# Keeping the weight rooms across a phase change, and starting loads, transposes and last sums at other places, in a one-core decoder layer

## The chip, the cores and the metric

One Trainium2 chip, one of its cores. The time is that of one launch in device microseconds (us); a lower time is better. Five engines work side by side, each through its own instructions in order: TensorE (PE in the profile, with PEld for its weight loads), VectorE (DVE), ScalarE (ACT), GpSimd (POOL) and SyncE (SP). SP computes nothing here: it issues loads from DRAM, one after the other. POOL computes a little and issues most stores. All transfers run on the same 16 DMA engines.

## The reference, cut to what matters

One decoder layer, in fp32, for a prompt of 2048 rows of 1024 columns and for a small group of samples (8 requests of 4 new rows each, with states and caches that are read from DRAM).

```python
def decoder_layer(x, s_gla, s_ssm, conv_buf, mk, mv, lw):
    m, s_gla, s_ssm, conv_buf = mixer(rmsnorm(x, lw['ln_mix_pre']), s_gla, s_ssm, conv_buf, lw)
    h = x + rmsnorm(m, lw['ln_mix_post'])
    a = cross_attend(rmsnorm(h, lw['ln_xa_pre']), mk, mv, lw['w_xq'], lw['w_xo'])
    h = h + rmsnorm(a, lw['ln_xa_post'])
    hf = rmsnorm(h, lw['ln_ffn_pre'])
    f = (jax.nn.silu(hf @ lw['w_gate']) * (hf @ lw['w_up'])) @ lw['w_down']
    h = h + rmsnorm(f, lw['ln_ffn_post'])
    return h, s_gla, s_ssm, conv_buf
```

The mixer (`mixer`) is an input projection, a gated linear attention, an SSD scan with a short convolution, and an output projection `w_out`. The attention (`cross_attend`) projects with `w_xq`, takes a softmax over 256 memory rows of 4 heads, and projects with `w_xo`. The feed-forward part has 2816 columns.

## The kernel before, in words

**Two phases.** Phase A (up to about 886 us) is the mixer without its output projection, in four blocks of 512 rows, and it leaves the mixed rows in DRAM (`mixT`). Phase B is everything behind it, and nearly all of the change lies there.

**Phase B is a row of passes.** `o` is the output projection, `s` the scores (with the query projection folded into the memory keys), `v` the values (folded with `w_xo`), each of 8 units, one for 256 rows. Then three passes `g` (gate and up projections, for three blocks of rows; 22 units each, one for 256 columns of gate or of up) and four passes `d` (parts of the down projection, 8 units each). A unit is one 2x2 block product by the Strassen-Winograd scheme: seven block products, in the order p0, C11, p3, p2, C12, C22, C21. In this text a unit is named by its pass and number, so g0.00 is the first unit of the first `g` pass, and one of its seven products is a *place*. At each place the kernel first emits the product's matmuls (12 for four inner blocks, three for each, because every fp32 operand is split into a high and a low half: L127 high x high, L128 and L129 the cross terms), into accA, accB or accC, and then the small steps that belong to other work.

**What a product needs.** The operand that PE loads as its weights comes from `Unit`: SP loads 1 MB or less into one of two `raw` buffers (L1521, L1530), DVE makes the Strassen sums (L1489), ACT the high half (L1507) and DVE the low half (L1509), four places ahead. The operand that streams comes from `Pieces`: it is loaded through three `st` buffers, and made into a high half by ACT (L1571, `r<-st`) and a low half by DVE (L1575), in *rooms* r0 to r6 (r7 too in `d`). A pass makes its seven products once and uses them in all its units, so a room comes free at the last unit of the pass, one at each place, and the next pass's pieces are made there ("coming").

**The rooms before.** In `o`, `s` and `v` a room has 2 x 2048 fp32 in each partition, in `g` and `d` 2 x 1536. `change_rooms` closes the pool "rx" and opens the pool "rf" of the smaller ones after the last product of v0.07. So no piece of g0 is made during v0.07 (`p = None` there), and g0.00 makes two pieces at each place.

**Work beside the products.** `posts` are generators that carry the rows of a finished unit on: `after_mix`, `after_scores`, `after_values` (norms, the residual, and `turned`: eight transposes on PE, L1691, of the rows `u` that ACT makes at L1730), `after_down` and `after_direct`. All are stepped once at each place (`tick`). `aux` and `back` hold side work that is stepped at so many tenths of a place (RATES): in `aux` `weight_sums` (Strassen sums of the next passes' weights: two loads on SP, then DVE L1410 to L1414, then stores on POOL) and `samples_down` (the down projection of the samples, with loads `w`), in `back` `samples` (mixer, states and attention of the samples, in g0 and g1). `pin` keeps each engine's instructions of phase B in the order in which this code is written, so a wait at the head of an engine's queue holds up all that is written behind it.

**The end.** In the last two units, d3.06 and d3.07, the sums of the other parts and the residual rows (`yp`, `hX`: two tensors of 512 KB for each 128 rows) are loaded by SP into free rooms when d3.06 begins (z and h), and added when the products are taken out of the accumulators (L1876). The unit before still adds by accumulating DMAs on POOL. Result rows `y` are a ring of 7 buffers.

## Time and profile before

| what | value |
|---|---|
| time, median of 3 runs | 3017.38 us (3011.25 to 3018.79) |
| profiled execution | 3010.56 us, its span 3008.8 us, mean TensorE clock 0.98 |
| instructions in the span | 42293 |
| PE busy | 2842.5 us, 94% of the span |
| DVE, ACT, POOL busy | 2086.4, 1523.9, 551.9 us |
| bytes moved | 529.89 MB, a mean of 176 GB/s |

How to read what is quoted below. A line of the *waits* names an engine and its line, the work that it waited for, and then the sum of the waits in us, their number, and the longest. A line of the *windows* gives a stretch of time in us and its length; then the busy time and the number of instructions of PE, PEld, DVE, ACT and POOL; then the clock that PE was granted (1.00 is full speed), the mean busy share of the 16 DMA engines, and GB/s. A line of a *timeline* gives the start, the length, the engine, the line and operation, the tile written and the tile read. A line of the *DMA issues* gives the number, the KB of one and the median us from issue to landing. Since PE is busy for 94% of the span, a stall is to be looked for in a stretch, not in the average.

### The profile page before, as it was taken

The numbers are of one execution on the slowest core, as the hardware profiler recorded it, in microseconds if no ns is written. First come the engines' busy times: TensorE is split into PE (matmuls) and PEld (weight loads), VectorE is DVE, ScalarE is ACT, GpSimd is POOL, SyncE is SP. The second block draws the span as 40 slices with busy tenths as digits, with TensorE's granted clock in tenths as the row PEclk, the third lists the DMA queues.
The fourth block names the chain that finished last, engine by engine and source line by source line (L and its number), as shares of the span: only waits on it lengthen the run. The fifth ranks groups of instructions, "written<-read, shape, count | busy, mean of one in ns | idle before, by whom it ended". The sixth has DMA issues, their size and how long they took to land.

```text
span 3008.8 us, 42293 instructions
## 1 busy us (share of the span) xinstructions
PE 2842.5 (94%) x15207; PEld 2385.9 (79%) x15207; DVE 2086.4 (69%) x3915; ACT 1523.9 (51%) x3044; POOL 551.9 (18%) x753
## 2 busy tenths in 40 slices
PE   8999989999988989999698999999999999999997
PEld 8887777787866778877588988888999995587875
DVE  7676676766657687777587777767678884566576
ACT  5454543645356686767544434434455552445453
POOL 2142341211222221034213000010000000011122
PEclk9999999999999999999799999999999999999998
DMA  7355543242267675567556356774243345768788
GB/s 247 115 157 171 166 129 117 78 130 85 88 221 251 222 262 199 189 192 236 186 194 216 136 176 215 256 262 142 96 154 119 127 144 180 243 130 196 161 214 244
DMA packets 154769, 529.89 MB, mean 176 GB/s; under 512 B 19360, under 2 KB 22608, under 8 KB 143040
## 3 DMA queue, kind: packets, MB, share of 16 engines
q1 hardware_dynamic: 93168, 331.75, 34.4%
q0 software_dynamic: 49152, 170.46, 18.6%
q10 hardware_dynamic: 12240, 24.99, 2.6%
q8 instruction: 120, 1.97, 0.3%
q14 instruction: 89, 0.73, 0.1%
HBM read 373.04 MB, written 154.09 MB: 175 GB/s over the span
## 4 chain that ended last, share of the span: by engine, by line
PE 56%; issue 16%; DMA 7%; DVE 6%; ACT 5%; POOL 2%; POOLq 0%; DVEq 0%; ACTq 0%; SPq 0%
PE accA L127 7%; PE accA L128 7%; PE accA L129 7%; PE accC L127 4%; PE acc L127 4%; PE accC L128 4%; PE accC L129 4%; PE acc L128 4%; PE acc L129 4%; PE accB L127 2%; PE accB L128 2%; PE accB L129 2%; PE mx L1916 1%; PE mx L1691 1%; ACT r L1571 1%
## 5 line engine op out<-in xcount | busy, mean ns | idle before, releaser
L127 PE MATMUL accA<-r,s 128*128 128x512 f32 (+2 forms) x1792 | 643.5, 359 | 39.5 <-ACT r L1571 13.5
L129 PE MATMUL accA<-r,s 128*128 128x512 f32 (+2 forms) x1792 | 631.7, 353 | 7.7 <-DVE s L1509 7.0
L128 PE MATMUL accA<-r,s 128*128 128x512 f32 (+2 forms) x1792 | 632.2, 353 | 6.9 <-DVE r L1575 6.8
L127 PEld LDWEIGHTS accA<-r,s 128*128 128x128 f32 x1792 | 340.5, 190 | 115.8 <-ACT r L1571 18.1
L1507 ACT ACTIVATE s<-sum 128x512 fp32r<-128x512 f32 (+2 forms) x488 | 289.4, 593 | 264.1 <-DVE sum L1489 102.0
L128 PEld LDWEIGHTS accA<-r,s 128*128 128x128 f32 x1792 | 340.7, 190 | 40.9 <-DVE r L1575 12.0
L129 PEld LDWEIGHTS accA<-r,s 128*128 128x128 f32 x1792 | 340.7, 190 | 39.2 <-DVE s L1509 9.6
L127 PE MATMUL accC<-r,s 128*128 128x512 f32 (+2 forms) x896 | 324.9, 363 | 18.7 <-ACT r L1571 6.8
L1509 DVE TENSOR_TENSOR s<-sum,s 128x512 fp32r<-128x512 f32 (+2 forms) x488 | 309.2, 642 | 35.0 <-ACT s L1507 31.7
L129 PE MATMUL accC<-r,s 128*128 128x512 f32 (+2 forms) x896 | 317.8, 355 | 7.4 <-DVE s L1509 7.4
L128 PE MATMUL accC<-r,s 128*128 128x512 f32 (+2 forms) x896 | 317.4, 354 | 1.0 <-DVE r L1575 0.9
L1509 DVE TENSOR_TENSOR s<-raw,s 128x512 fp32r<-128x512 f32 (+2 forms) x366 | 235.4, 643 | 59.0 <-ACT s L1507 57.5
L1507 ACT ACTIVATE s<-raw 128x512 fp32r<-128x512 f32 (+2 forms) x366 | 218.2, 596 | 53.2 <-PE accC L129 50.9
L121 ACT ACTIVATE whi<-wraw 128x1024 fp32r<-128x1024 f32 (+2 forms) x148 | 137.1, 941 | 197.1 <-PE acc L128 100.2
L127 PEld LDWEIGHTS accC<-r,s 128*128 128x128 f32 x896 | 171.5, 191 | 63.0 <-issue 11.2
L122 DVE TENSOR_TENSOR wlo<-wraw,whi 128x1024 fp32r<-128x1024 f32 (+2 forms) x148 | 167.5, 1142 | 59.2 <-ACT whi L121 58.5
L129 PEld LDWEIGHTS accC<-r,s 128*128 128x128 f32 x896 | 171.7, 192 | 25.1 <-DVE s L1509 9.1
L1575 DVE TENSOR_TENSOR r<-st,r 128x1024 fp32r<-128x1024 f32 (+2 forms) x133 | 136.6, 1029 | 76.1 <-ACT r L1571 75.6
L128 PEld LDWEIGHTS accC<-r,s 128*128 128x128 f32 x896 | 171.7, 192 | 16.7 <-DVE r L1575 2.1
L127 PE MATMUL acc<-xh,whi 128*128 128x512 f32 (+1 forms) x464 | 168.3, 364 | 8.4 <-ACT xh L282 8.3
L135 POOL TENSOR_TENSOR rs<-ms,nhalf 128x1 f32<-128x1 f32 (+4 forms) x125 | 105.8, 848 | 329.2 <-DVE ms L133 322.1
L129 PE MATMUL acc<-xh,wlo 128*128 128x512 f32 (+1 forms) x464 | 164.2, 355 | 1.7 <-DVE wlo L122 1.7
(644 smaller groups left out, 5775.4 us busy)
## 6 DMA issues: line engine op xcount, KB each, us to landing
raw<-in_w_gu_dram SPq DMA_DIRECT2D x66, 1024.0 KB, 5.0
wraw<-in_w_in_fm_dram SPq DMA_DIRECT2D x52, 512.0 KB, 3.7
wraw<-in_w_in_tm_dram SPq DMA_DIRECT2D x48, 512.0 KB, 3.7
yp<-y POOLq DMA_DIRECT2D x48, 512.0 KB, 6.8
raw<-aT SPq DMA_DIRECT2D x24, 768.0 KB, 5.2
st<-in_w_down_dram SPq DMA_DIRECT2D x34, 512.0 KB, 6.9
aT<-og POOLq DMA_DIRECT2D x22, 768.0 KB, 4.3
hX<-y POOLq DMA_DIRECT2D x32, 512.0 KB, 5.4
```

What stands on the lines that cost most here:

```text
L121: last[0] = nc.scalar.activation(hi[:, cs], raw[:, cs], AF.Copy)
L122: nc.vector.tensor_tensor(lo[:, cs], raw[:, cs], f(hi)[:, cs], op=ALU.subtract)
L127: nc.tensor.matmul(ps, lhsT=wh, rhs=ah, start=start, stop=False, skip_group_check=more)
L128: nc.tensor.matmul(ps, lhsT=wh, rhs=al, start=False, stop=False, skip_group_check=more)
L129: nc.tensor.matmul(ps, lhsT=wl, rhs=ah, start=False, stop=stop, skip_group_check=more)
L135: nc.gpsimd.tensor_tensor(out=rs[:rows, :cols], in0=ms[:rows, :cols], in1=nhalf[:rows, :cols], op=ALU.pow)
L1507: nc.scalar.activation(h3, v, AF.Copy)
L1509: return lambda: nc.vector.tensor_tensor(l3, v, f(h3), op=ALU.subtract)
L1571: nc.scalar.activation(hi, v, AF.Copy)
L1575: nc.vector.tensor_tensor(lo, v, f(hi), op=ALU.subtract)
L1691: nc.tensor.transpose(ps[kt // 4][:, kt % 4 * P:(kt % 4 + 1) * P], u[:, kt * P:(kt + 1) * P], ident)
L1916: nc.tensor.matmul(ps[g0:g0 + 32], lhsT=s_f[:, kt].rearrange("p h t -> p (h t)"), rhs=ws.popleft(), start=kt < 4, stop=kt >= FT - 4, tile_ ...
```

## The change

Every part of the change moves, keeps or splits work; the matmuls are the same in number and size.

- **Rooms.** `change_rooms` is gone. One pool "rp" of seven rooms of 2 x 1536 stays open for all of phase B. In `o`, `s` and `v`, whose halves need 2048, the missing 1024 of each room stand in a second tile `e` in the pool "rx", which is closed when g0 begins (the `wide` form). Pieces of g0 are made during v0.07, one at each place, like those of any other pass.
- **Transposes.** `after_mix` and `after_values` yield once more before `turned`, and the ring `u` has four buffers in place of three.
- **weight_sums** yields four times in place of two between its loads and its sums.
- **Samples.** `back` is stepped at 6 tenths of a place in `g` instead of 5. The convolution state is loaded earlier, and the convolution is split by yields. The sample value rows go through DRAM (`svs`) instead of staying in a buffer. The loads of `cache_k` and `cache_v` are issued two ahead.
- **d0.** When `d` begins, its pool places the room r7 and the five `w` buffers first, so that the tiles which follow lie elsewhere: `y` no longer lies where `og` (the output tile of `g`) was, and the first `w` buffer does. So ScalarE's first write of `y` (L1878) waits for PE alone, and SP's first `w` load (L1905) waits for the stores of `og`; before it was the other way round.
- **The end.** All eight loads of `yp` and `hX` are issued when d3.05 begins.

```diff
+    rp = ctx.enter_context(tc.tile_pool(name="rp", bufs=1, reuse_waits="tile"))
+    rx = rctx.enter_context(tc.tile_pool(name="rx", bufs=1, reuse_waits="tile"))
...
-    RW = 2048
+    RW = 1536
@@ weight_sums
-        yield
-        yield
+        for _ in range(4):
+            yield
@@ Pieces.larger
-                self.at[i] = r[:, 0:RW], r[:, RW:2 * RW]
+                if self.wide:
+
+                    e = rx.tile([P, 1024], F32R, name=f"e{k}")
+                    self.at[i] = [r[:, c * 1024:(c + 1) * 1024] for c in range(2)], [r[:, 2048:3072], e]
+                else:
+                    self.at[i] = r[:, 0:RW], r[:, RW:2 * RW]
@@ after_mix
         u = yield from after_rows(j, m, y, ss, "ln_mix_post", a["x"])
+        yield
         turned(u)
@@ after_values
         u = yield from after_rows(j, m, y, ss, "ln_xa_post", None)
+        yield
         turned(u, gff)
@@ sample_mixer
+        cvo = mt_([P, 8, NR, 3], "cvo")
+        nc.gpsimd.dma_start(out=cvo, in_=a["state_conv"])
+        yield
+        yield
+        yield
...
-        cvo = mt_([P, 8, NR, 3], "cvo")
-        nc.gpsimd.dma_start(out=cvo, in_=a["state_conv"])
+        yield
...
+            if i % 2:
+                yield
@@ the passes
-    RATES = {"o": (0, 9), "s": (0, 9), "v": (0, 0), "g": (5, 4), "d": (0, 8)}
+    RATES = {"o": (0, 9), "s": (0, 9), "v": (0, 0), "g": (6, 4), "d": (0, 8)}
@@ enter
         if kind == "g":
             if i == 0:
+                rctx.close()
                 pg = fctx.enter_context(tc.tile_pool(name="pg", bufs=1, reuse_waits="tile"))
...
             pd = ctx.enter_context(tc.tile_pool(name="pd", bufs=1, reuse_waits="tile"))
+
+            pd.tile([P, 2 * RW], F32R, name="r7")
+            pd.tile([P, 512], F32, name="w", bufs=5)
             gain_row(pd, "ln_ffn_post")
@@ the loop over the products
-                if n + 2 >= len(work):
-
-                    if n + 2 == len(work):
+                if n + 3 == len(work):
...
+                    for j in (g + 1, g + 2):
+                        z, h = [rooms.pop(0), rooms.pop(0)], [rooms.pop(0), rooms.pop(0)]
+                        for m in range(2):
+                            nc.sync.dma_start(out=z[m], in_=yp[j][:, m * D:(m + 1) * D])
+                            nc.sync.dma_start(out=h[m], in_=hX[rows(j, m)])
...
-        if i == 6 and n + 1 < len(work) and begins[n + 1] and k + 1 == XG:
-            change_rooms()
-            for _ in range(2):
-                coming.step()
...
-        if p and p is coming and work[cur][0] + 1 == XG:
-            p = None
         if p:
             p.larger()
         tick()
         if p:
             p.smaller()
-            if p.k == XG:
-                p.step()
```

**ScalarE, from the end of v0.07 into g0.00.** `r<-st` are the pieces of g0 (two to a product, the number is that of the room's tile), `sg<-accA` is the first product of g0.00 taken out, `u<-y` the rows that are transposed next, and `u<-mx` the transposed rows read back. Before:

```order
L1682 ACTIVATE mx,sq_13168<-y 128x512
L1507 ACTIVATE s<-sum 128x512
L1698 ACTIVATE u<-mx,cols 128x128 x4
L1571 ACTIVATE r_13301<-st 128x4x256
L1571 ACTIVATE r_13301<-st 128x4x128
L1676 COPY y<-accA 128x512
L1682 ACTIVATE mx,sq_13168<-y 128x512
L1507 ACTIVATE s<-sum 128x512
L1724 ACTIVATE mx,ss<-y 128x512 x2
L1795 COPY sg<-accA 128x384
L1507 ACTIVATE s<-sum 128x512
L1571 ACTIVATE r_13359<-st 128x4x256
```

Now (L1609 is the former L1571, L1837 the former L1795):

```order
L1609 ACTIVATE r_13323<-st 128x4x256
L1716 COPY y<-accA 128x512
L1722 ACTIVATE mx,sq_13208<-y 128x512
L1540 ACTIVATE s<-sum 128x512
L1609 ACTIVATE r_13323<-st 128x4x128
L1738 ACTIVATE u<-mx,cols 128x128 x4
L1764 ACTIVATE mx,ss<-y 128x512 x2
L1837 COPY sg<-accA 128x384
L1540 ACTIVATE s<-sum 128x512
L1609 ACTIVATE r_13403<-st 128x4x256
```

Before, the pieces of one product stood ahead of the first `sg`; now those of four do (r_13323 is the fourth), and one piece stands at each place instead of two.

**VectorE in the `o` pass, the second of its weight sums.** `st<-st` are the sums of `weight_sums`, `s` and `sum` the operands of the coming products, `y<-y,u` the residual. Before:

```order
L1509 TENSOR_TENSOR s<-sum,s 128x512
L1489 TENSOR_TENSOR sum<-raw 128x512
L1658 SCALAR_TENSOR_TENSOR y<-y,rs,ga 128x1024
L1410 TENSOR_TENSOR st<-st 128x512
L1411 TENSOR_TENSOR st<-st 128x512
L1678 TENSOR_TENSOR y<-accB,y 128x512
L1509 TENSOR_TENSOR s<-sum,s 128x512
```

Now:

```order
L1718 TENSOR_TENSOR y<-accA,y 128x512
L1542 TENSOR_TENSOR s<-raw,s 128x512
L1522 TENSOR_TENSOR sum<-sum,raw 128x512
L1443 TENSOR_TENSOR st<-st 128x512
L1444 TENSOR_TENSOR st<-st 128x512
L1542 TENSOR_TENSOR s<-sum,s 128x512
L1522 TENSOR_TENSOR sum<-raw,sum 128x512
```

The second pair of sums stood 20 instructions behind the first before and stands 30 behind it now, and the first itself stands nine later.

**SyncE at the end.** `raw<-aT` are the loads of the last units' operands, the eight loads of `yp` and `hX` the last sums and residual rows. Before:

```order
L1605 DMA st<-wT 128x512
L1530 DMA raw<-aT 128x1536 x6
L2085 DMA r_27223<-yp 128x1024
L2086 DMA r_27223<-hX 128x1024
L2085 DMA r_27223<-yp 128x1024
L2086 DMA m<-hX 128x1024
L2085 DMA st<-yp 128x1024
```

Now:

```order
L1645 DMA st<-wT 128x512
L1563 DMA raw<-aT 128x1536 x5
L2122 DMA r_27114<-yp 128x1024
L2123 DMA r_27114<-hX 128x1024
L2122 DMA r_27114<-yp 128x1024
L2123 DMA m<-hX 128x1024
L2122 DMA st<-yp 128x1024
L2123 DMA st<-hX 128x1024
L2122 DMA st<-yp 128x1024
L2123 DMA y<-hX 128x1024
L1563 DMA raw<-aT 128x1536
```

The eight loads stand ahead of the last `raw` now, and behind it before.

85 lines of the change are left out of this document (50 added, 35 removed).

## The prediction

> **What bounds the kernel now.** I read the page's totals first, then the waits of PE over the whole span, then windows cut at the units of phase B. The totals:
>
> ```profile
> span 3008.8 us, 42293 instructions
> PE 2842.5 (94%) x15207; PEld 2385.9 (79%) x15207; DVE 2086.4 (69%) x3915; ACT 1523.9 (51%) x3044; POOL 551.9 (18%) x753
> ```
>
> PE is busy for all but 166 us, and the change removes no matmul. So it can only earn idle time of PE, and the half-clock stretches beside it. Where that idle time lies, by what ended it:
>
> ```profile
> PE mx L1691 <- ACT u L1730: 21.8, 28, 5.3
> PE accA L127 <- ACT r L1571: 13.5, 8, 4.2
> PE accA L127 <- DVE sps L155: 6.3, 1, 6.3
> PE accA L127 <- ACT y L1878: 5.3, 2, 4.6
> ```
>
> The transposes, the first pieces of g0, one sample step and the first result tile of d0 are all places that the change touches. The windows give the price of each stretch:
>
> ```profile
> 943.00:997.80 54.80, 45.91 (x201) 36.92 (x201) 38.24 (x70) 31.97 (x71) 18.33 (x30) 0.94 0.83 287
> 998.00:1063.90 65.90, 63.70 (x302) 51.69 (x301) 43.91 (x74) 45.54 (x98) 15.25 (x23) 1.00 0.60 210
> 1063.90:1113.50 49.60, 42.52 (x201) 34.52 (x200) 43.39 (x64) 41.90 (x76) 10.60 (x16) 1.00 0.83 286
> 1113.50:1239.40 125.90, 125.90 (x608) 105.24 (x607) 87.26 (x153) 84.84 (x213) 16.05 (x29) 1.00 0.52 187
> 1282.70:1414.30 131.60, 126.13 (x587) 102.14 (x586) 94.48 (x172) 89.44 (x210) 52.16 (x76) 1.00 0.69 209
> 1414.30:1436.90 22.60, 21.46 (x102) 17.08 (x100) 15.18 (x29) 17.07 (x40) 9.94 (x15) 1.00 0.85 251
> 1436.90:1489.00 52.10, 28.90 (x101) 24.29 (x101) 27.32 (x44) 24.54 (x48) 10.07 (x15) 0.71 0.56 174
> 1489.00:1508.80 19.80, 18.70 (x100) 17.81 (x101) 14.54 (x28) 12.43 (x29) 6.74 (x11) 0.91 0.49 178
> 1508.80:1531.00 22.20, 15.40 (x87) 14.49 (x85) 19.73 (x69) 10.14 (x19) 6.55 (x12) 0.94 0.69 249
> 1531.00:1550.20 19.20, 19.13 (x104) 17.49 (x105) 17.15 (x53) 10.76 (x21) 2.17 (x4) 0.89 0.25 85
> 2880.50:2952.00 71.50, 71.50 (x315) 59.18 (x316) 50.62 (x100) 37.94 (x91) 24.45 (x34) 1.00 0.96 228
> 2952.00:2976.40 24.40, 18.33 (x73) 14.43 (x72) 13.33 (x26) 10.18 (x27) 5.27 (x8) 0.93 1.04 324
> 2976.40:3008.80 32.40, 16.31 (x55) 11.10 (x54) 20.66 (x34) 4.88 (x14) 6.15 (x10) 0.80 0.53 172
> ```
>
> In order these are o0.02 and o0.03; o0.04 to o0.06; o0.07 and s0.00; six units of `s`; v0.01 to v0.06; v0.07; g0.00; g0.01; g0.02; g0.03; five units of d3; d3.06; d3.07 with the tail. The six units of `s` are the yardstick: PE is never idle, 125.9/6 = 20.98 us for a unit with its transposes.
>
> **The change part by part.** *Rooms.* g0.00 takes 52.1 us where g0.01, with one matmul fewer, takes 19.8. Its waits:
>
> ```profile
> PE accA L127 <- ACT r L1571: 9.2, 4, 4.2
> PE accC L127 <- ACT r L1571: 6.8, 2, 4.2
> ```
>
> These 16 us, and PE's half clock (0.71), come from making 14 pieces inside one unit. Now seven are made in v0.07, one at each place, and seven in g0.00. The work is moved, not removed, so I add up v0.07, g0.00 and g0.01: 94.5 us before. Three floors hold. PE: 21.0 + 18.8 + 18.7 = 58.5 us. DVE: 15.18 + 27.32 + 14.54 = 57.0 us. DMA: 22.6 x 251 + 52.1 x 174 + 19.8 x 178 GB/s = 18.3 MB, which at the highest rate above (324 GB/s) is 56 us. Three engines within 3 us of each other do not mesh perfectly, so I take 67 us and a gain of 27. The best case is 36 (the PE floor). The worst I allow is 15, half of what is stalled.
>
> The clock column has to be right for this: 0.71 in g0.00, whose longest single waits on pieces are 4.2 us, against 1.00 in o0.04 to o0.06, whose 2.2 idle us come in short waits (0.65 us, worked out below). [...]
>
> *Transposes.* One more place between `u` and the transposes is what `s` has already, with no idle time. The row L1691 says 21.8 us in 28 waits. Of these, a few belong to the next item:
>
> ```profile
> PE mx L1691 <- ACT u L1730: 6.3, 4, 5.3
> DVE st L1410 <- DMA st<-wqk: 11.5, 2, 6.6
> ```
>
> Both rows are of 943 to 998. The rest, 15.5 us, is 0.65 us a wait. I take back what the windows show idle: 65.9 - 63.7 = 2.2 for o0.04 to o0.06, 4.5 of 5.5 for v0.01 to v0.06, 0.5 for o0.01, and 4 of 7.1 at o0.07 and s0.00, where DVE alone has 43.4 us of work. That is 11; bounds 7 and 15.5. The fourth `u` buffer pays for the row that now lives a place longer; without it ACT's write of `u` would wait, and the operands behind it.
>
> *weight_sums.* Twice DVE stood in its queue for a load of `wqk`, 11.5 us together, and behind it stood the operands of the next products. Side work is stepped at 9 tenths of a place of 3.0 us here, so two more steps are 6.7 us of lead, and the longest wait was 6.6. The two units are 54.8 - 2 x 20.98 = 12.8 us over the yardstick. But 54.8 x 287 GB/s = 15.7 MB, and at 324 GB/s that is 48.5 us, a gain of 6.3 unless the sums that move behind o0.03 take their bytes along. I take 8; bounds 4 and 12.8. Each later pair of loads is only issued some places later, so SP waits for nothing new.
>
> *Sample steps.* g0.02 waits 6.3 us for the sample's `sps`. DVE's timeline shows why: the convolution stands in one piece ahead of it.
>
> ```profile
> 1524.09 0.49 DVE L989 TENSOR_SCALAR cvs<-s_xbc,cols 128x32 f32<-128x32 f32 x2
> 1528.67 1.04 DVE L991 SCALAR_TENSOR_TENSOR cvs<-s_xbc,cols,cvs 128x32 f32<-128x32 f32 x6
> 1529.64 0.15 DVE L153 TENSOR_SCALAR sps<-spe 32x8 f32<-32x8 f32 x1
> ```
>
> From 1524.1 to 1529.7 DVE runs four such pairs of rows, 32 steps, and its operand for the next product is late. Split by yields the steps lie between operands. What goes is 6.3 us, the 0.94 clock of g0.02 (15.4 x 0.06 = 0.9) and the 0.89 of g0.03 (19.1 x 0.11 = 2.1): 9.3. DVE has 19.7 of 22.2 us of work in that window, so I allow 4 as the worst and 9.3 as the best, and take 9. The cache loads two ahead meet a PE that is busy there: 0, up to 2.
>
> *Rate 6.* Steps come every 1.67 places instead of 2, so in units of some 17 us (2.4 us a place) each has 0.8 us less. The state loops depend on it:
>
> ```profile
> SPq L976 <- DMA out_ssm_s_dram<-Ms: 31.3, 5, 13.5
> PE accA L129 <- DVE s L1509: 4.0, 1, 4.0
> ```
>
> The first row (1585 to 1662) is SP waiting for a state room whose store has not landed, with the `raw` loads queued behind; the second (1618 to 1660) is what PE saw of it. Eight such rooms at 0.8 us would be 6.5 us more, a longer lead for the other loads could be 4 less. I take a loss of 1.
>
> *d0.* The wait that is to go:
>
> ```profile
> ACT y L1878 <- DMA aT<-og: 6.6, 1, 6.6
> 2487.23 0.73 POOL L1825 DMA_DIRECT2D aT<-og  x1 [25.14 <-DVE s_f L1823]
> 2490.10 0.39 PE L129 MATMUL accC<-r,s 128*128 128x512 f32 x1
> 2495.07 0.80 PE L127 MATMUL accA<-r,s 128*128 128x512 f32 x1 [4.58 <-ACT y L1878]
> aT<-og POOLq DMA_DIRECT2D x1, 512.0 KB, 7.0
> aT<-og POOLq DMA_DIRECT2D x22, 768.0 KB, 4.3
> DMA to landing us min/median/max: 2.5/5.8/8.8
> ```
>
> The last row is of the `w` loads (L1905). They now wait for the same store of `og`, and the first sample matmul stands in PE's queue right behind the third place, where PE stops at 2490.1. The store landed 7.0 us after its issue, at 2494.2, with five `w` beside it; without them it may take the 4.3 us that the larger ones take, so 2491.5. A `w` lands 2.5 to 5.8 later: 2494.0 to 2500.0, against 2495.1 now. The wait goes from ACT to SP and PE: between a gain of 1.1 and a loss of 5; I take a loss of 1.
>
> *The end.* d3.06 takes 24.4 us where 71.5/5 = 14.3 is steady, and these are the waits behind it:
>
> ```profile
> 2935.10 14.60 SPq L1530 DMA_DIRECT2D raw<-aT  x2
> 2949.80 0.43 SPq L2085 DMA_DIRECT2D r<-yp  x1
> DVE y L1876 <- DMA r<-yp: 9.0, 2, 7.9
> DVE y L1876 <- DMA out_y_dram<-y: 3.9, 1, 3.9
> ```
>
> The loads stood behind the last `raw`, which itself waited until about 2949. They now go ahead of it, some 12 us earlier, so the 7.9 us wait can end. But the eight are 8 x 512 KB = 4.2 MB, 13 us of all queues at 324 GB/s, and the share is 0.96 before and 1.04 there: the result stores, whose buffers DVE waits for next (the 3.9 us row), land later for it. One of the eight takes a `y` buffer a unit earlier, too. Best 10 (all the excess), worst a loss of 3; I take 3.
>
> Sum: 27 + 11 + 8 + 9 - 1 - 1 + 3 = 56. The profiled execution, 3010.56 us, would be 2955; its median stands 6.8 higher, 3017.38, and gives **2961**.
>
> **The rivals.**
>
> *DMA binds where PE was stalled.* Everything that gains is pressed into less time with the same bytes. For it: the shares 0.85 in v0.07 at 251 GB/s (295 at a full share, so 18.3 MB need 62 us, and late loads stall as before), 0.83 in o0.02 and o0.03, above 1 at the end. Against it: 0.56 in g0.00. Then rooms give 18, `weight_sums` 4, the end nothing, d0 a loss of 3: 18 + 11 + 4 + 9 - 1 - 3 = 38, 2979 us. [...]
>
> *All of it comes in.* Rooms 34, transposes 14, `weight_sums` 12, samples 9, the end 8: 77, 2940 us. For it: in `s` PE shows no idle time at all under the same load. Against: DVE at 57.0 of 58.5 us in the transition.
>
> *The stalls only move.* Pieces of g0 stand in v0.07, but their loads come after `raw` loads in SP's queue and three `st` buffers, so they are late one place further on; transposes wait for another ACT instruction. Then rooms 6, transposes 4, `weight_sums` 2, samples 5: 17, 3000 us. Against it: the other passes make their pieces in this way, and s0.00 and v0 show no such wait above.
>
> *Slower: state rooms at 6 tenths.* SP is blocked by the next state load until a store has landed (31.3 us in five waits), and `raw` stands behind it. There are 32 state loads (16 of each kind). To be slower than before, each would have to cost PE 56/32 = 1.8 us more than now, where the rows above give 4.0 us for five, 0.8 each; at 2.2 us it is 70 lost and 3031 us. For it: 0.8 us less for each step. Against: of SP's 31 us PE saw 4.
>
> **How the numbers follow.** Forecast 0.62, DMA bound 0.17, all of it 0.12, only moved 0.06, slower 0.03. The forecast's own range is 2946 to 2978, from the bounds of its terms taken as independent. The range reaches to 2938 and 2990: it leaves out the two last rivals and a part of the tails. About 9 us (0.3%) is what a measurement of this kernel can tell from no change, so faster means below 3008: 0.95; within it 0.02; slower 0.03.
>
> **What would show it.** g0.00 at 20 to 23 us with a clock above 0.9, and no wait on `r` above 2 us there (rooms); v0.07 at 21 to 24 us. The row "mx <- ACT u" at a few us in place of 21.8. No DVE wait on `st<-wqk`, and o0.02 with o0.03 at 42 to 49 us. No 6.3 us wait on `sps`. In d0.00 a PE wait for `w` of 3 to 9 us in place of the one for `y`. At the end no 7.9 us wait on `r<-yp`, but one on `out_y` of 4 us or more. I am wrong if v0.07 to g0.01 together stay above 80 us, or if a DMA share near 1 stands beside PE waits there.

## The result and the profile after

The changed kernel takes 2966.11 us (median of four runs, 2964.11 to 2969.38), the kernel before 3016.89 us beside it. The ratio is 0.9836, with a 95% interval of 0.9819 to 0.9853: 1.6% faster. The prediction was 2961 us, with a range of 2938 to 2990. The whole came out 5 us above the forecast, but two of its seven terms were off by more than that, both with the wrong sign, and part of the closeness is luck (see below).

The totals of the changed kernel's page:

```profile
span 2964.2 us, 42292 instructions
PE 2830.4 (95%) x15207; PEld 2385.0 (80%) x15207; DVE 2089.2 (70%) x3915; ACT 1526.3 (51%) x3047; POOL 554.2 (19%) x754
```

The waits of PE over its whole span:

```profile
PE accC L125 <- ACT y L1920: 15.9, 3, 7.2
PE accA L125 <- ACT r L1609: 6.8, 6, 2.1
PE mx L1731 <- ACT u L1770: 6.4, 4, 4.8
PE accC L125 <- DVE y L1918: 6.3, 2, 4.1
PE mx L1118 <- DVE sBm L1115: 4.8, 1, 4.8
```

The line numbers have moved: L125 to L127 are the three matmuls of a product (before L127 to L129), L1731 the transposes, L1609 the pieces, L1540 and L1542 the operands, L1920 and L1918 the result tiles of d. The transposes' wait has shrunk from 21.8 us in 28 to 6.4 in 4, the one of accA on pieces from 13.5 us to 6.8, the one on `sps` is gone. At the head there is now a wait on `y` that was 2 us before: 7.2 us of it in d3.05, the other two, of 4.1 and 4.6 us, in the first units of d2 and d3. The same stretches as in the prediction, cut at the same units:

```profile
943.50:985.50 42.00, 41.94 (x204) 34.87 (x202) 34.30 (x62) 29.54 (x65) 15.99 (x26) 1.00 0.87 301
985.50:1048.40 62.90, 62.84 (x304) 52.29 (x301) 48.34 (x86) 46.72 (x104) 19.85 (x30) 1.00 0.76 275
1286.30:1390.40 104.10, 104.10 (x500) 86.99 (x499) 78.66 (x147) 77.12 (x183) 51.69 (x70) 1.00 0.76 227
1390.40:1416.90 26.50, 22.83 (x103) 18.35 (x102) 20.15 (x35) 19.36 (x44) 10.25 (x15) 0.94 0.99 320
1416.90:1445.10 28.20, 21.06 (x103) 20.13 (x102) 22.51 (x38) 21.83 (x45) 10.08 (x15) 0.82 0.80 244
1445.10:1461.70 16.60, 16.60 (x103) 16.38 (x102) 14.64 (x29) 12.65 (x32) 6.41 (x10) 1.00 0.60 209
2436.80:2453.60 16.80, 15.27 (x52) 8.77 (x50) 8.75 (x20) 6.17 (x13) 1.29 (x2) 0.94 0.51 161
2829.40:2886.50 57.10, 57.10 (x254) 47.28 (x253) 40.01 (x79) 30.26 (x72) 18.62 (x26) 1.00 0.93 219
2886.50:2910.40 23.90, 16.71 (x64) 13.29 (x63) 10.45 (x21) 7.72 (x19) 5.64 (x8) 0.86 1.04 325
2910.40:2930.60 20.20, 16.15 (x64) 12.92 (x63) 12.19 (x24) 8.35 (x22) 4.80 (x7) 0.92 0.84 231
```

In order: o0.02 and o0.03; o0.04 to o0.06; v0.02 to v0.06; v0.07; g0.00; g0.01; d0.00; d3.01 to d3.04; d3.05; d3.06. The o and v units run at the yardstick now (42.0/2 = 21.0, 62.9/3 = 21.0, 104.1/5 = 20.8 us, PE idle for 0.1 us or less). g0.00 has gone from 52.1 to 28.2 us. d3.05, which took the steady 14.3 us before, takes 23.9. And the sample stretch, from g0.02 to g1.14, before:

```profile
1508.80:2133.90 625.10, 604.81 (x3527) 535.62 (x3526) 456.01 (x880) 268.21 (x499) 73.93 (x110) 0.99 0.57 195
```

and in the changed kernel:

```profile
1461.70:2083.30 621.60, 608.52 (x3527) 537.41 (x3526) 460.06 (x880) 270.76 (x502) 69.68 (x111) 0.99 0.58 197
```

Where the 44.6 us between the two profiled spans come from, by such stretches (us; the terms are those of the prediction):

| stretch | before | after | gain | predicted |
|---|---|---|---|---|
| v0.07 to g0.01 (rooms) | 94.5 | 71.3 | 23.2 | 27 |
| o0.01, o0.04 to o0.06, o0.07 to s0.01, v0.02 to v0.06 (transposes) | 271.0 | 258.5 | 12.5 | 11 |
| o0.02 and o0.03 (weight_sums) | 54.8 | 42.0 | 12.8 | 8 |
| g0.02 to g1.14 (sample steps, rate) | 625.1 | 621.6 | 3.5 | 9 - 1 |
| d0.00 | 21.9 | 16.8 | 5.1 | -1 |
| d3.05 to the last matmul (the end) | 61.0 | 67.7 | -6.7 | 3 |
| all the rest | 1880.5 | 1886.3 | -5.8 | 0 |

The rest is spread thin: 1 us in phase A, 0.7 in o0.00, 2.4 from g1.15 to g2.21, 2.1 from d0.01 to d3.04, where the first units of d2 and d3 are 1.5 and 1.9 us longer with the two waits on `y` above; each in one execution.

### The profile page after: what moved, and what is told of

It reads as the page before. It is cut to its first block, busy times and chain, and to the rows that moved or that the text cites. A ratio compares the mean times of both kernels' runs of the same rounds, so it can differ in the third digit from the quotient of the medians.

```text
span 2964.2 us, 42292 instructions
## 1 busy us (share of the span) xinstructions
PE 2830.4 (95%) x15207; PEld 2385.0 (80%) x15207; DVE 2089.2 (70%) x3915; ACT 1526.3 (51%) x3047; POOL 554.2 (19%) x754
## 4 chain that ended last, share of the span: by engine, by line
PE 49%; issue 25%; DVE 7%; DMA 5%; ACT 4%; POOL 2%; POOLq 0%; DVEq 0%; ACTq 0%; SPq 0%
PE accA L125 6%; PE accA L126 6%; PE accA L127 6%; PE acc L125 4%; PE acc L126 4%; PE acc L127 4%; PE accC L125 3%; PE accC L127 3%; PE accC L126 3%; PE accB L125 1%; PE mx L1958 1%; PE accB L127 1%; PE accB L126 1%; DVE s L1542 1%; ACT r L1609 1%
## 5 line engine op out<-in xcount | busy, mean ns | idle before, releaser
L125 PE MATMUL accA<-r,s 128*128 128x512 f32 (+2 forms) x1792 | 643.6, 359 | 27.3 <-ACT r L1609 6.8
L127 PE MATMUL accA<-r,s 128*128 128x512 f32 (+2 forms) x1792 | 631.6, 352 | 2.0 <-DVE s L1542 1.9
L126 PE MATMUL accA<-r,s 128*128 128x384 f32 (+2 forms) x1600 | 556.6, 348 | 1.8 <-DVE r L1613 1.8
L125 PEld LDWEIGHTS accA<-r,s 128*128 128x128 f32 x1792 | 340.8, 190 | 103.4 <-issue 24.2
L1540 ACT ACTIVATE s<-sum 128x512 fp32r<-128x512 f32 (+2 forms) x488 | 289.0, 593 | 249.4 <-DVE sum L1522 103.2
L127 PEld LDWEIGHTS accA<-r,s 128*128 128x128 f32 x1792 | 341.0, 190 | 35.2 <-DVE s L1542 3.6
L125 PE MATMUL accC<-r,s 128*128 128x512 f32 (+2 forms) x896 | 322.7, 360 | 27.2 <-ACT y L1920 15.9
L1542 DVE TENSOR_TENSOR s<-sum,s 128x512 fp32r<-128x512 f32 (+2 forms) x488 | 310.6, 644 | 29.6 <-ACT s L1540 23.6
L126 PEld LDWEIGHTS accA<-r,s 128*128 128x128 f32 x1600 | 304.7, 190 | 25.4 <-DVE r L1613 3.9
L127 PE MATMUL accC<-r,s 128*128 128x512 f32 (+2 forms) x896 | 315.8, 352 | 0.2 <-DVE s L1542 0.2
L1542 DVE TENSOR_TENSOR s<-raw,s 128x512 fp32r<-128x512 f32 (+2 forms) x366 | 236.0, 645 | 70.5 <-ACT s L1540 69.2
L126 PE MATMUL accC<-r,s 128*128 128x384 f32 (+2 forms) x800 | 277.9, 347 | 0.3 <-DVE r L1613 0.3
L1540 ACT ACTIVATE s<-raw 128x512 fp32r<-128x512 f32 (+2 forms) x366 | 218.2, 596 | 64.8 <-PE accC L127 59.2
L125 PEld LDWEIGHTS accC<-r,s 128*128 128x128 f32 x896 | 170.4, 190 | 67.7 <-ACT y L1920 22.2
L127 PEld LDWEIGHTS accC<-r,s 128*128 128x128 f32 x896 | 170.2, 190 | 16.9 <-DVE s L1542 0.9
L125 PE MATMUL acc<-xh,whi 128*128 128x512 f32 (+1 forms) x464 | 168.7, 365 | 8.4 <-ACT xh L280 8.2
L133 POOL TENSOR_TENSOR rs<-ms,nhalf 128x1 f32<-128x1 f32 (+4 forms) x125 | 113.9, 913 | 329.2 <-DVE ms L131 312.9
L127 PE MATMUL acc<-xh,wlo 128*128 128x512 f32 (+1 forms) x464 | 164.9, 357 | 1.7 <-DVE wlo L120 1.7
L126 PE MATMUL acc<-xl,whi 128*128 128x512 f32 (+1 forms) x464 | 164.4, 356 | 0.2 <-DVE xl L281 0.2
L126 PEld LDWEIGHTS accC<-r,s 128*128 128x128 f32 x800 | 152.7, 191 | 10.7 <-DVE r L1613 0.6
```

The costliest lines, as they stand in the source:

```text
L125: nc.tensor.matmul(ps, lhsT=wh, rhs=ah, start=start, stop=False, skip_group_check=more)
L126: nc.tensor.matmul(ps, lhsT=wh, rhs=al, start=False, stop=False, skip_group_check=more)
L127: nc.tensor.matmul(ps, lhsT=wl, rhs=ah, start=False, stop=stop, skip_group_check=more)
L133: nc.gpsimd.tensor_tensor(out=rs[:rows, :cols], in0=ms[:rows, :cols], in1=nhalf[:rows, :cols], op=ALU.pow)
L1540: nc.scalar.activation(h3, v, AF.Copy)
L1542: return lambda: nc.vector.tensor_tensor(l3, v, f(h3), op=ALU.subtract)
```

## The experiments

All were timed beside the kernel before on the same chip. That kernel's medians on these occasions lie between 3012.59 and 3016.89 us, so a difference to the changed kernel is given by the medians and, where that differs, by the ratios too. Only the first experiment and the last three have an interval of the ratio wholly outside that of the changed kernel (0.9819 to 0.9853). For the others the stretches carry the reading.

The stretches quoted come from one profiled execution of each kernel, but they repeat from kernel to kernel: v0.07 to g0.01 takes 70.8 to 74.8 us in all kernels with the new rooms (66.5 with fewer bytes), v0.02 to v0.06 takes 104.1 or 104.2 in all with the later transposes, o0.02 and o0.03 take 42.0 to 44.0 in all with four yields, and d3.05 takes 23.2 to 24.9 in the eight kernels that issue all eight loads there and 14.3 in the five that do not.

**The rooms alone undone.**

```diff
-    rp = ctx.enter_context(tc.tile_pool(name="rp", bufs=1, reuse_waits="tile"))
-    rx = rctx.enter_context(tc.tile_pool(name="rx", bufs=1, reuse_waits="tile"))
+    rp = rctx.enter_context(tc.tile_pool(name="rx", bufs=1, reuse_waits="tile"))
...
-    RW = 1536
+    RW = 2048
...
+        if i == 6 and n + 1 < len(work) and begins[n + 1] and k + 1 == XG:
+            change_rooms()
+            for _ in range(2):
+                coming.step()
...
+        if p and p is coming and work[cur][0] + 1 == XG:
+            p = None
...
+            if p.k == XG:
+                p.step()
```

> The changed kernel with only the rooms as before: one pool of large rooms that is closed after v0.07 and a pool of smaller ones opened, no piece of g0 in v0.07, two at each place in g0.00. Theory (the pieces of g0, all made in one unit, are the stall): v0.07 to g0.01 take 90 to 95 us together as before (94.6) where the changed kernel takes 71.3, g0.00 above 45 us at a clock near 0.7; 20 to 26 us slower than the changed kernel, 2986 to 2992 us. Rival (transposes a place later in v and the smaller load of that stretch relieve it anyway, the rooms are worth little): v0.07 to g0.01 below 80 us, under 2975 us.

Measured: 2982.49 us, ratio to before 0.9903 (0.9886 to 0.9919), so 16 us slower than the changed kernel (20 by the ratios). Windows of v0.07, g0.00 and g0.01, and PE's waits for pieces in the first two:

```profile
1389.90:1411.90 22.00, 21.22 (x104) 17.39 (x102) 16.43 (x31) 17.09 (x40) 10.89 (x15) 1.00 0.95 291
1411.90:1461.30 49.40, 28.72 (x103) 24.27 (x101) 25.86 (x42) 24.07 (x47) 9.74 (x15) 0.65 0.63 200
1461.30:1479.00 17.70, 16.75 (x100) 16.39 (x101) 15.75 (x30) 13.21 (x33) 6.41 (x10) 1.00 0.42 142
...
PE accA L125 <- ACT r L1608: 8.0, 2, 4.2
PE accC L125 <- ACT r L1608: 7.1, 2, 4.4
```

g0.00 is back at 49.4 us with a clock of 0.65, and the three units take 89.1 us in place of 71.3. The theory holds, with 17.8 us in the stretch in place of 20 to 26: the other parts of the change shorten this stretch by some 5 us without the rooms.

**The place of the transposes undone.**

```diff
         u = yield from after_rows(j, m, y, ss, "ln_mix_post", a["x"])
-        yield
         turned(u)
...
         u = yield from after_rows(j, m, y, ss, "ln_xa_post", None)
-        yield
         turned(u, gff)
```

> The changed kernel without the additional yield ahead of the transposes in after_mix and after_values (the fourth u buffer stays). Theory (each transpose waits some 0.65 us for the row that ScalarE has just made): PE's waits on u come back to 14 to 20 us in 24 or more waits, o0.04 to o0.06 at 22.0 us a unit and v0.02 to v0.06 at 22.1 in place of 20.9; 9 to 14 us slower than the changed kernel, 2975 to 2980 us. Rival (it was the late weight sums that made ScalarE late, and with them gone the transposes are in time): waits on u stay under 8 us, the units at 20.9, less than 4 us slower.

Measured: 2971.46 us, ratio 0.9865 (0.9850 to 0.9879), 5 us slower (9 by the ratios). PE's wait:

```profile
PE mx L1731 <- ACT u L1770: 29.4, 30, 6.7
```

The windows of o0.04 to o0.06 and of v0.02 to v0.06:

```profile
989.70:1055.70 66.00, 63.80 (x301) 51.80 (x300) 48.50 (x85) 47.08 (x104) 20.53 (x31) 1.00 0.73 262
1296.00:1406.60 110.60, 106.40 (x502) 86.36 (x501) 79.78 (x149) 77.59 (x185) 47.84 (x70) 1.00 0.73 223
```

The waits are back (30 of them), and the units are at 22.0 and 22.1 us again although the weight sums are in time: the rival falls. The stretches of o, s and v lose 16 us against the changed kernel (1.2 in o0.01, 2.1 in o0.02 and o0.03, 3.2, 2.8 at o0.07 to s0.01, 6.4), more than the 9 to 14 expected; the whole time only loses 5 to 9. In this execution the sample stretch took 611.2 us in place of 621.6, and d0 and the first units of d2 and d3 some 5 us less; why, this run does not show. The fourth `u` buffer stayed in it, so what that buffer is worth is not shown either.

**weight_sums with two yields again.**

```diff
-        for _ in range(4):
+        for _ in range(2):
             yield
```

> The changed kernel with two yields in weight_sums instead of four. Theory (VectorE stood in its queue for the loads of wqk, and the operands of the next products behind it): waits of VectorE on st<-wqk of 8 to 13 us are back, o0.02 and o0.03 take 50 to 55 us in place of 42.0; 8 to 13 us slower, 2974 to 2979 us. Rival (DMA is full there, so the two units were slow by their bytes and the sums only moved them on): o0.02 and o0.03 at 42 to 46 us, under 4 us slower.

Measured: 2972.81 us, ratio 0.9865 (0.9849 to 0.9882), 7 us slower (9 by the ratios). VectorE's wait from 940 to 1000:

```profile
DVE st L1443 <- DMA st<-wqk: 10.6, 2, 6.3
```

The window of o0.02 and o0.03:

```profile
942.90:993.30 50.40, 44.19 (x204) 35.97 (x202) 36.61 (x65) 30.11 (x68) 17.37 (x28) 0.96 0.84 297
```

The two waits on `wqk` are back and 8.4 of the 12.8 us with them; of the other 4.4, undoing the transposes had brought back 2.1. The limit of bytes that the prediction set here (48.5 us for 15.7 MB) is no limit: the changed kernel moves 42.0 x 301 GB/s = 12.6 MB in these units, with PE busy throughout. The rest of the bytes has moved to the units behind, where the share rose from 0.60 to 0.76.

**The end as before.**

```diff
-                if n + 3 == len(work):
+                z = h = None
+                if n + 2 >= len(work):
+
+                    if n + 2 == len(work):
...
-                    for j in (g + 1, g + 2):
-                        z, h = [rooms.pop(0), rooms.pop(0)], [rooms.pop(0), rooms.pop(0)]
-                        for m in range(2):
-                            nc.sync.dma_start(out=z[m], in_=yp[j][:, m * D:(m + 1) * D])
-                            nc.sync.dma_start(out=h[m], in_=hX[rows(j, m)])
-                        adds.append((z, h))
+                    z, h = [rooms.pop(0), rooms.pop(0)], [rooms.pop(0), rooms.pop(0)]
+                    for m in range(2):
+                        nc.sync.dma_start(out=z[m], in_=yp[g][:, m * D:(m + 1) * D])
+                        nc.sync.dma_start(out=h[m], in_=hX[rows(g, m)])
```

> The changed kernel with the eight loads of yp and hX as before, four when d3.06 begins and four when d3.07 begins. Theory (loading all eight when d3.05 begins takes a y buffer a unit early and adds 4.2 MB to queues that are full, so ScalarE's first writes of y in d3.05 wait for result stores, 5.95 and 6.64 us): d3.05 back from 23.9 to 14.3 us, d3.06 up from 20.2 to about 22.4; 5 to 9 us faster than the changed kernel, 2957 to 2961 us. Rival (d3.05 is slow for another reason, such as the pace of the whole pass by then): d3.05 above 20 us, the same time within 3 us or slower.

Measured: 2958.22 us, ratio 0.9822 (0.9803 to 0.9841), 8 us faster than the changed kernel by the medians, 4 by the ratios. As in the kernel before, four of the eight loads go out when d3.06 begins and four when d3.07 begins. First, what ScalarE waited for in d3.05 of the changed kernel, from its timeline:

```profile
2891.16 0.59 ACT L1920 COPY y<-accA 128x512 f32<-128x512 f32 x1 [5.95 <-DMA out_y_dram<-y]
...
2901.36 0.59 ACT L1920 COPY y<-accC 128x512 f32<-128x512 f32 x1 [6.64 <-DMA out_y_dram<-y]
```

Then the windows of d3.05 and d3.06 with the loads at their old places:

```profile
2893.30:2907.60 14.30, 14.30 (x64) 11.82 (x63) 10.36 (x21) 7.84 (x19) 5.64 (x8) 1.00 1.06 276
2907.60:2929.60 22.00, 16.25 (x65) 12.73 (x64) 12.14 (x24) 8.37 (x22) 4.79 (x7) 0.92 1.04 329
```

d3.05 is at PE's pace again, and d3.06 loses 1.8 us. From d3.05 to the last matmul it is 60.8 us in place of 67.7, so this part of the change costs 7 us in its stretch. ScalarE wants a free `y` buffer, the ring has one less from d3.05 on, and the store that frees it lands later with the loads beside it: the median from issue to landing of a result store was 8.6 us in the 44 us before d3.05 and 12.4 in the stretch from 2884 to 2911, of the early `st<-yp` loads 23.3. Which of the two counts for more, the missing buffer or the late store, no run separates; but full queues alone do not slow the unit, since d3.05 runs here without a pause of PE at a DMA share of 1.06. The views of the changed kernel:

```profile
out_y_dram<-y POOLq DMA_DIRECT2D x5, 512.0 KB, 8.6
...
st<-yp SPq DMA_DIRECT2D x2, 512.0 KB, 23.3
...
out_y_dram<-y POOLq DMA_DIRECT2D x2, 512.0 KB, 12.4
```

**The sample work at 5 tenths.**

```diff
-    RATES = {..., "g": (6, 4), ...}
+    RATES = {..., "g": (5, 4), ...}
```

> The changed kernel with the sample work stepped at 5 tenths of a place in the g passes, as before. The sample stretch (the units from g0.02 to g1.14) took 625.1 us before and takes 621.6 in the changed kernel, a gain of 3.5 where the splitting of the convolution alone was to give 9. Theory (the quicker step gives back what the splitting gains, since the state loads wait for stores): the stretch at 612 to 618 us, no wait of PE on sBm near 4.8 us in g0.08 to g0.11; 4 to 9 us faster than the changed kernel. Rival (the stalls fall where loads and stores happen to meet, and the rate only moves them): the stretch at 619 to 627 us, within 3 us of the changed kernel.

Measured: 2958.80 us, ratio 0.9815 (0.9799 to 0.9832), 7 us faster than the changed kernel (6 by the ratios). The stretch:

```profile
1462.50:2077.90 615.40, 602.46 (x3510) 534.37 (x3509) 451.42 (x863) 262.83 (x490) 63.85 (x101) 0.99 0.57 198
```

6.2 us less, of which 1.6 are 16 small matmuls that now come after it. The longest wait on `sBm` is 1.7 us. From g0.02 to the end of g2 the eight kernels here that have the step at 6 tenths and the same code in this stretch take 965.2 to 978.7 us, with a mean of 972.7; the three at 5 tenths (two of them below) take 968.8 to 970.6, with a mean of 969.6. So the quicker step costs 3 us by the stretches and 6 or 7 by the times of this run. All of them point to a loss, but the intervals overlap, and the eight kernels lie 13.5 us apart among themselves: its size is not settled. Nor is its way: SyncE's waits for the stores of the states come to 46.5 us in the changed kernel's stretch and 42.9 here, those at the loads of `cache_v` (L1331) to 11.6 and 1.7, and no run shows which of them PE pays. What the cache loads two ahead are worth by themselves, which the prediction put at nothing, no run separates either.

**The convolution in one piece again, at 5 tenths.**

```diff
-        cvo = mt_([P, 8, NR, 3], "cvo")
-        nc.gpsimd.dma_start(out=cvo, in_=a["state_conv"])
-        yield
-        yield
-        yield
...
+        cvo = mt_([P, 8, NR, 3], "cvo")
+        nc.gpsimd.dma_start(out=cvo, in_=a["state_conv"])
...
-            if i % 2:
-                yield
...
-    RATES = {..., "g": (6, 4), ...}
+    RATES = {..., "g": (5, 4), ...}
```

> The changed kernel with the step at 5 tenths and the convolution of the samples in one piece again, its state loaded where it was. Beside the run with the step at 5 tenths alone (the stretch from g0.02 to g1.14 at 615.5 us) this prices the splitting by itself. Theory: the 6.3 us wait on sps and the half clock behind it are back in g0.02 or g0.03, the stretch at 622 to 626 us, 6 to 10 us slower than with the step at 5 tenths alone, 2965 to 2969 us. Rival (the wait was an effect of the late start of g0.02 behind the slow g0.00): no wait of PE on sps above 2 us, the stretch at 614 to 618 us.

Measured: 2968.51 us, ratio 0.9848 (0.9832 to 0.9864), 10 us slower than with the step at 5 tenths alone. The stretch:

```profile
1460.00:2081.00 621.00, 603.41 (x3520) 533.67 (x3519) 456.14 (x875) 267.89 (x499) 69.43 (x106) 0.99 0.57 197
```

PE's wait:

```profile
PE accA L125 <- DVE sps L153: 7.1, 1, 7.1
```

The wait on `sps` is back, 7.1 us, after a g0.00 that is as quick as in the changed kernel. The splitting is worth 5.6 us in the stretch (some 0.8 of it are eight small matmuls that stand in it here and behind it there) and 10 in the time, about what the prediction had (9).

**Without the two tiles at the head of d's pool.**

```diff
-            pd.tile([P, 2 * RW], F32R, name="r7")
-            pd.tile([P, 512], F32, name="w", bufs=5)
```

> The changed kernel without the two tiles that are placed first in the pool of d, so that y lies on og again and ScalarE waits for its store. Theory (the wait on the store is worth more at y than at w, because five w loads then run beside the store and it lands 7.0 us after its issue instead of 3.1): d0.00 back from 16.8 to 20 to 22 us with a wait of ScalarE on og of 5 to 7 us; 3 to 5 us slower. Rival (the wait only moves, as the prediction had it): d0.00 at 16 to 18 us, no difference.

Measured: 2963.04 us, ratio 0.9838 (0.9819 to 0.9856). The window of d0.00 in the kernel before, then here:

```profile
2485.10:2507.00 21.90, 17.32 (x50) 10.13 (x50) 9.65 (x20) 5.44 (x12) 1.30 (x2) 0.79 0.41 138
...
2433.20:2452.60 19.40, 17.11 (x52) 9.33 (x51) 8.44 (x19) 6.00 (x13) 1.28 (x2) 0.85 0.57 166
```

ScalarE's wait here, and PE's wait in the changed kernel:

```profile
ACT y L1920 <- DMA aT<-og: 6.5, 1, 6.5
...
PE mx L1958 <- DMA w<-in_w_down_dram: 1.5, 1, 1.5
```

The old wait is back and d0.00 takes 2.6 us more, half of what the stretch had gained. The other half no run shows; what differs from the kernel before is that the store of `og` is issued 0.9 us after the unit begins instead of 2.1, and that PE waits 1.2 us for `y` instead of 4.6. In the whole time, 3 us under the changed kernel by the medians and 1 above it by the ratios, with overlapping intervals, it does not show.

**Fewer bytes around v0.07.**

```diff
-            add_rows(y, hX[rows(j, m)])
+            if j < 5:
+                add_rows(y, hX[rows(j, m)])
```

> The changed kernel, where after_values leaves out the residual hX of the last three units of v (their rows of the result are without it, and 3.1 MB of accumulating loads are gone around v0.06 to g0.00; nothing else is). Theory (the 12.8 us that v0.07 to g0.01 still take over PE's floor of 58.5 come from full DMA queues, share 0.99 in v0.07, so that the loads of xp land late): v0.07 to g0.01 at 62 to 67 us in place of 71.3, waits on st<-xp under half of the 10 us they have in v0.07 and g0.00. Rival (VectorE and ScalarE in order are the limit: 57 us of VectorE's work in three units): 70 to 73 us. In both cases the whole time follows by the same amount, within 3 us.

This kernel leaves the residual out of three units' rows and nothing else. Measured: 2958.81 us, ratio 0.9818 (0.9803 to 0.9833), 7 us less (5 by the ratios). Windows of v0.07 and g0.00:

```profile
1390.60:1417.20 26.60, 22.94 (x103) 18.40 (x101) 21.91 (x38) 20.77 (x45) 8.49 (x13) 0.94 0.73 272
1417.20:1440.00 22.80, 18.68 (x102) 17.51 (x100) 20.03 (x35) 19.97 (x42) 7.94 (x13) 0.93 0.66 214
```

ScalarE's wait on the loads of `xp` in both together:

```profile
ACT r L1609 <- DMA st<-xp: 1.4, 2, 1.0
```

In the changed kernel these waits are longer (6.7 us in two; the expectation's 10 counts one of them twice), and PE stands in this stretch as follows:

```profile
ACT r L1609 <- DMA st<-xp: 6.7, 2, 3.6
...
PE mx L1731 <- ACT u L1770: 5.0, 2, 4.8
PE accA L125 <- DVE y L1718: 3.4, 1, 3.4
```

Both sides hold in part. g0.00 falls from 28.2 to 22.8 us, and the wait of PE on `u` from 4.8 to 2.3: in the changed kernel ScalarE stood 3.6 us for a load of `xp` just ahead of g0.00, VectorE 4.9 us behind it for the piece, and the row `u` came at the end of that backlog. Neither ScalarE nor GpSimd waits there for the residual loads themselves, but the loads `st<-xp` that are issued from 1400 to 1412 land after 9.5 us in the changed kernel and 6.4 here (median of three of 512 KB), so it is the bytes that count. v0.07 keeps its 26.6 us although the DMA share falls from 0.99 to 0.73: its 3.4 us wait is VectorE's, which makes the pieces and then takes the product out. Of the 12.8 us over PE's floor some 5 go with these bytes.

**Another end.**

```diff
...
+                if b == 2 and n + 4 + NJ == len(work):
+                    hm = pd.tile([P, D], F32, name="m")
+                    hw = [[pd.tile([P, 512], F32, name="w", bufs=5) for _ in range(2)] for _ in range(2)]
+                    nc.sync.dma_start(out=hm, in_=hX[rows(NJ - 2, 0)])
...
                 if n + 3 == len(work):
...
-                    rooms = [r[:, c * D:(c + 1) * D] for c in range(3)] + [pd.tile([P, D], F32, name="m")]
-                    rooms += [stage() for _ in range(3)] + [pd.tile([P, D], F32, name="y", bufs=7)]
+                    rooms = [r[:, c * D:(c + 1) * D] for c in range(3)] + [stage() for _ in range(2)]
+                    for m in range(2):
+                        nc.sync.dma_start(out=rooms[m], in_=yp[g + 1][:, m * D:(m + 1) * D])
+                if n + 2 == len(work):
...
+                    nc.sync.dma_start(out=rooms[4], in_=hX[rows(g + 1, 1)])
```

> The changed kernel with another end: three of the four residual row tiles hX of d3.06 and d3.07 are loaded in the middle of d2, into the rooms m and w that are free then; the sums yp of d3.06 are loaded when d3.05 begins; the other three loads when d3.06 begins; no y buffer is taken. Theory (the end is bound by bytes in full queues and by the y ring, so fewer bytes there, and no y buffer, let both units run at PE's pace): d3.05 at 14.3 us, d3.06 at 15 to 19 us, d3.07 at 20 to 23; 9 to 15 us faster than the changed kernel, 2951 to 2957 us. Rival (what d3.06 waits for is the result stores of the units before, which are late whatever is loaded): d3.06 stays at 20 to 22 us, 5 to 8 us faster, as with the loads back at their old places.

Measured: 2952.25 us, ratio 0.9796 (0.9782 to 0.9811), 14 us faster than the changed kernel (12 by the ratios). Windows of d3.05 and d3.06:

```profile
2883.60:2897.90 14.30, 14.30 (x65) 11.84 (x64) 10.28 (x20) 7.96 (x19) 4.05 (x6) 1.00 1.05 310
2897.90:2919.20 21.30, 17.28 (x64) 13.76 (x63) 12.41 (x24) 8.21 (x22) 6.74 (x10) 0.84 1.05 291
```

VectorE's timeline in d3.06, where it waits 2.9 us before the norm of an earlier unit's rows:

```profile
2908.19 1.28 DVE L1698 SCALAR_TENSOR_TENSOR y<-y,rs,ga 128x1024 f32<-128x1024 f32 x1 [2.92 <-POOL rs L133]
```

d3.05 to the last matmul takes 56.8 us in place of 67.7. The time is the theory's, but the way is not: d3.06 stays at 21.3 us, and the gain over the old places of the loads is in d3.07 (21.1 us against 24.5).

**All that the runs pointed to, together.** The other end, the step at 5 tenths, and this:

```diff
-        yield from pause(6)
+        yield from pause(9 if j == NJ - 3 else 6)
```

> The changed kernel with what the runs so far point to: the step at 5 tenths, three residual tiles loaded in the middle of d2 and no y buffer taken for the last sums, and after_down of the rows of d3.05 three places later, since VectorE stood there 2.9 us for its norm, behind an accumulating load that took 13 us, with the additions of d3.06 queued behind. Theory: the terms add up, 2966 - 11 for the end, - 6 for the rate, - 4 for d3.06 (15 to 18 us in place of 21.4): 2945 us, 2942 to 2949. Rival (the later norm meets d3.07 instead, and rate and end are not independent): d3.06 at 15 to 18 but d3.07 above 24 us, or 2949 to 2954 us.

Measured: 2948.37 us, ratio 0.9777 (0.9761 to 0.9794). Its interval lies wholly below that of the changed kernel (0.9819 to 0.9853), so this version beats both; that of "Another end" it overlaps. d3.06 takes 20.0 us, so the last term failed: the tile whose norm VectorE still waited for was of d3.04. One more run gave that one the pause too:

```diff
-        yield from pause(9 if j == NJ - 3 else 6)
+        yield from pause(9 if j >= NJ - 4 else 6)
```

> As the last version, with the later norm for the rows of d3.04 too: the VectorE wait of 2.92 us in d3.06 there was for a tile of d3.04, whose accumulating load took 14.3 us, and not of d3.05. Theory: that wait is gone, d3.06 at 14.5 to 17 us in place of 20.0; 3 to 6 us faster than that version, 2942 to 2946 us. Rival (the queues are full, so whatever stands there waits, and the result stores are only later): d3.06 or d3.07 longer by as much, within 2 us of 2948.

Measured: 2949.02 us, ratio 0.9786 (0.9772 to 0.9799). The window of d3.06:

```profile
2890.20:2908.80 18.60, 16.07 (x65) 12.85 (x64) 11.70 (x23) 7.74 (x20) 4.48 (x7) 0.91 1.04 299
```

1.4 us less in d3.06, 3.0 more in d3.07, the same time. The rival holds: VectorE's waits for its norm in the last units come to 4.7 us in the run before and 4.1 in this one, so the wait has changed its place. That d3.06 and d3.07 are bound by their bytes (the share in d3.06 is 1.04 to 1.05 in four of the five ends) is argued, not shown: a run that takes bytes away there was not made. For d3.05 the bytes alone are not the limit, since it runs at PE's pace at the same share in four of the five.

## Why the prediction was right, and where it was not

**Rooms: right, 4 us too much.** The mechanism is shown by the first experiment. The sum of floors (PE 58.5, VectorE 57.0, DMA 56) named the right limits, and 67 us was 4 too hopeful: the stretch came out at 71.3 us, and the two causes that the prediction set beside each other as forecast and rival, VectorE in order and full queues, are both in it, with about 5 us that go with the bytes. The three signs named for it: v0.07 between 21 and 24 us (it took 26.5), g0.00 between 20 and 23 at a clock above 0.9 (28.2 at 0.82), no wait on `r` above 2 us (2.1). The first two missed clearly, the third by 0.1. And one of the signs of being wrong came: a DMA share of 0.99 in v0.07 beside a PE wait of 3.4 us. The run with fewer bytes has the same wait at a share of 0.73, and in the first experiment, with no pieces in v0.07, it is 0.8 us at a share of 0.95: VectorE's order makes it, not the queues.

The clock, too, was taken too simply. The 27 us for the rooms, with 18.8 us of PE for g0.00, and the sign of a clock above 0.9 count on a clock that comes back once the waits are short; no run shows how short they have to be. What the runs show is this. In the changed kernel g0.00 has waits of 4.8 and 2.1 us and a clock of 0.82: behind the first it is 0.50 from 1431.87 to 1435.21, behind the second 0.50 from 1439.02 to 1442.20. g0.01 has no wait and 1.00. In the run with fewer bytes the longest wait of g0.00 is 2.3 us, and behind it the matmuls begin every 0.32 us instead of every 0.17, for some 3 us, which is the 0.93 of that unit:

```profile
1425.24 0.33 PE L126 MATMUL accA<-r,s 128*128 128x384 f32 x1
1425.41 0.34 PE L127 MATMUL accA<-r,s 128*128 128x384 f32 x1
1428.07 1.09 PE L1731 MATMUL mx<-ident,u 128*128 128x128 f32 x8 [2.32 <-ACT u L1771]
...
1429.67 0.52 PE L125 MATMUL accC<-r,s 128*128 128x384 f32 x1
1429.99 0.52 PE L126 MATMUL accC<-r,s 128*128 128x384 f32 x1
```

So here waits of 2.1 and 2.3 us were followed by half the clock, as the one of 4.8 us was; those of 0.5 us and less in o0.04 to o0.06 of the kernel before were not (clock 1.00).

**Transposes: right** (11 predicted, 12.5 measured). **weight_sums: too small** (8 against 12.8 in the two units; undone by itself, 8.4 of it comes back, and 2.1 belongs to the transposes). The step that failed is the bound by bytes: 48.5 us for the two units was worked out from the bytes that they moved before, but the change also moves the second pair of sums back, and the queues gave 301 GB/s without a wait of PE.

**Sample steps: right by itself; rate: mis-sized.** Split, the convolution gives 5 to 10 us (9 predicted), but the stretch gained only 3.5. The step "I take a loss of 1" for the rate is the likely one to have failed: the runs put it at 3 to 7 us, up to the bound of 6.5 that the prediction worked out and did not take. That the waits for the state stores are the way is not shown.

**d0: wrong sign** (a loss of 1 predicted, 5.1 gained in the stretch, 2.6 when it is undone). The wait did move from ScalarE to SP and PE as described. What failed is the time that the store takes once the five loads no longer run beside it: the prediction took 4.3 us from the larger stores, it was 3.1, and the first of the loads landed 2.5 us after that. The waits show one of PE on `w`, of 1.5 us, where 3 to 9 were expected.

**The end: wrong sign** (a gain of 3 predicted, a loss of 6.7 measured in the stretch, and 6.9 of it come back by undoing it). Both causes stand in the prediction, the `y` buffer that is taken a unit early and the 4.2 MB that the result stores have to wait for, but they were weighed as a worst case of 3. The step that failed is to have set the wait that ends (7.9 us) against a bound for the new one, and not to have followed the ring: the two writes of `y` in d3.05 each wait for a store, 5.95 and 6.64 us. The wait that was to end did end: no wait of VectorE on `r<-yp` is left. In the changed kernel, with SyncE's eight loads beside them at a share of 1.04, the stores that GpSimd issues landed after 12.4 us in place of 8.6.

**The rivals.** "DMA binds" came true in part at the end and in some 5 of the 12.8 us that are left over PE's floor in v0.07 to g0.01, not in o0.02 and o0.03. The slower case did not come. That the forecast came so close is partly luck. The errors were of both signs (`weight_sums` 5, d0 6 and the transposes 1.5 us too low; rooms 4, samples 4.5, the end 9.7 and the rest 5.8 too high), and they leave the sum 11 us too high: 56 predicted, 44.6 between the two profiled spans. The forecast missed by only 5 because the profiled execution of the kernel before was 6.8 us quicker than its median, which the prediction added, and that of the changed kernel (2965.97) was at its median.

## What to carry to other kernels

Where an operand ring is thrown away and rebuilt between two phases, keep it and put the excess of the wider phase into a second tile: here three units went from 94.5 us to 71.3, and 17.8 of that went again with the rooms alone. Before moving loads earlier, read the DMA share where they will land and follow the ring that they take a buffer from: here, at a share of 1.04, the result stores landed 3.8 us later, a buffer of their ring was taken a unit early, and ScalarE stood twice in the unit for a free `y`. A wait that moves from one engine to another may still be worth having, if what runs beside the awaited transfer changes with it: here d0.00 gained 5.1 us, and the store of `og` landed after 3.1 us in place of 7.0.

## What the runs showed of the hardware that was not expected

The store of `og` (512 KB) landed 3.1 us after its issue with no load issued beside it and 7.1 us with five loads of 256 KB and one of 512 KB beside it, as the DMA issues of the changed kernel and of the one without the two tiles show (the kernel before: 7.0):

```profile
aT<-og POOLq DMA_DIRECT2D x1, 512.0 KB, 3.1
```

```profile
aT<-og POOLq DMA_DIRECT2D x1, 512.0 KB, 7.1
```

So here the order of issue, not only the amount, set when the awaited transfer ended. And the sample stretch, with the same instructions in it, took between 611 and 625 us in the eight kernels that have it at 6 tenths, one execution of each; why, no run shows. So a difference of a few us there is not told apart by one profiled execution.
